# Hybrid trunk: input scaled as its chunks land, the unscaled transposes moved to the output projection, time steps from the normalised input

## Chip, core and metric

One core of one Trainium2 chip runs the whole forward pass in one launch. The metric is the device time of one execution in microseconds. The engines are PE (TensorE), DVE (VectorE), ACT (ScalarE), POOL (GpSimd) and SP (SyncE, which here only issues DMAs; ACT and POOL issue some as well).

## What is computed

The reference, cut to the part that the change touches. SEQ = 1024 tokens and 16 meta tokens ahead of them give L = 1040 rows of D = 1024; the mixer has 32 heads in 4 groups, an inner width of 2048, a state of 128.

```
h = concatenate([meta_tokens, x])                      # 1040 x 1024
u = rmsnorm(h) * ssd_norm
z, xbc, dt_raw = split(u @ w_in)                       # 2048, 2048 + 2*4*128, 32
xbc = silu(causal_conv4(xbc) + conv_b)
dt = softplus(dt_raw + dt_bias);  a = -exp(a_log)
y = chunked_state_space_scan(xbc, dt, a)               # scores cb, decays, states
hg = rmsnorm_per_group(y * silu(z)) * gate_norm
h = h + hg @ w_out                                     # the output projection
...                                                    # conv FFN; K/V; attention; conv FFN; final norm
```

All matrices are float32. A product at nearly full precision is made of three products of rounded operands (`mm3`): each operand is split into a high part rounded to fp32r and a low part, the rest, and high·high, high·low and low·high are summed in PSUM. In the names, `wh`/`wl` are the parts of a weight, `uh`/`ul` those of the normalised input, `yh`/`y` those of the gated scan's output.

## The kernel before

**Tiles.** The rows lie in 9 chunks of 116 (the last 112) tokens, `CH`; three chunks make one of the three time tiles of 348, 348 and 344 columns, `TT`. Features are handled as 8 blocks `k` of 128. After the transposition, features lie on partitions and tokens along the row.

**Front (`load_x`, L327 to L398).** SP and ACT issue the loads of the chunks in turn (L405; odd chunks and the meta tokens on SP, even ones on ACT), and SP that of the dt weight. For each time tile there are two steps, in the order of the table `ORD`. `stream(j)` squares the tile's chunks (L364 on DVE for the chunks in `SQD`, L366 on ACT), transposes the raw chunks (L371, `xT`), copies them out as the residual `hs` (L374 on ACT, L376 on DVE), multiplies them with the dt weight in full fp32 (L377, `dtr`), sends them to memory for the third tile (L379, `h_d`), and forms each row's normalising factor (`token_rstd`, L244 to L250: one step on DVE, Ln and Exp on ACT, four steps on DVE). `scaled(j)` multiplies the chunks by their factors in place (L388), transposes them again (L393, `xr`), and splits them with the norm's gain (`parts`: `uh` L303 on ACT, `ul` L304 on DVE).

**Projections and scan.** `stream` (L603) walks blocks of 128 output columns, three time tiles each: 24 products (`pj`, L193 to L195), then for the blocks that need it the convolution (ACT L320, DVE L323) and a silu that `settle` puts out later. The weight of a block is loaded by SP (L174), its high part made by ACT (L180), its low part by POOL (L98). `dt_path` (L434 to L503) makes the time steps and decay sums from `dtr` while group 0 is projected; it multiplies `dtr` by the rows' factors because `dtr` was made from unscaled input, and sends its tables `acs_d` and `ea_d` to memory, to be read back as `D` and `E`. The scan's first score is `cb` (L665).

**Output projection (`out_proj`, L817).** For groups g = 0, 1, 2 and output blocks f = 0 to 7, `accumulate` sums four `mm3` for each time tile into a bank `acc` and adds it to the residual `h[f]` on DVE (L431). Five banks go round. For g = 0, `fetch` (L419) reads `h[f]` back from `h_d`. For g = 1 and 2, `fetch_y` (L804) reads the group's output from memory and `split_y` scales and splits it (DVE t L813, ACT `yh` L814, DVE `y` L815); group 0's is split ahead by the same lines. At the same time the last group's gate norm ends: PE's column sums of squares `ms` (L226), ACT's Ln and Exp (L229, L230) and DVE's steps L231 to L234, then L579.

**Order.** A scheduler orders the instructions of every engine ahead of time, and the engines carry them out in that order. `behind(x, y)` adds an order only: x is put after y. Within a tile pool a name takes a bank or buffer when its last reader is done; `xT` in the changed kernel, `ms` and `xr` share three banks (`sm`). DMA completions of SP and ACT go through eight semaphores in turn, so a DMA is issued only when the one eight before it has ended.

## Time and profile before

| | |
|---|---|
| median of three runs | 2895.37 us (2894.5 to 2897.03) |
| the profiled execution | 2894.96 us, its span 2893.3 us |
| PE, DVE, ACT, POOL busy in the span | 2834.0, 2092.7, 1628.8, 1631.9 us |
| mean granted clock of PE | 0.996 |
| DMA | 278.70 MB, 96 GB/s over the span |

Busy time is what an engine spent on instructions that are not control or DMA issue. In rows of the timeline the first number is the start in us from the beginning of the span, the second the duration; "x3" is the number of instructions that were put together, and the bracket says how long the engine was idle before and what ended it. Durations of neighbours on one engine overlap where the engine is pipelined, so the step from one start to the next is the price in a row.

### The profile page before, as it was taken

To read this page: it belongs to the slowest core of one execution; us is meant where nothing else is said; L and a number is where in the kernel's file an instruction comes from. 1 tells how busy PE (TensorE), PEld (TensorE's weight loads), DVE (VectorE), ACT (ScalarE), POOL (GpSimd) and SP (SyncE) were. 2 spreads that over 40 slices of the span, in tenths; PEclk is the share of its full clock that TensorE was granted. 3 is DMA by queue.
4 is the path that set the end of the run, shared out by engine and by line. 5 is a ranking of instruction groups with operands and counts; after the bars stand their busy time and mean duration, and the time that the engine had idled before them with its cause. 6 is when DMAs were issued, how large, how long until landed. Compare 5 with 4: busy or idle time off the path is not lost.

```text
span 2893.3 us, 58596 instructions
## 1 busy us (share of the span) xinstructions
PE 2834.0 (98%) x21835; PEld 2704.3 (93%) x21835; DVE 2092.7 (72%) x4032; ACT 1628.8 (56%) x3386; POOL 1631.9 (56%) x2438
## 2 busy tenths in 40 slices
PE   7999999999999999999999999999998999999998
PEld 4999999999989999999999999999798999999888
DVE  5676666668387666667886888888749676767776
ACT  4455544544256555565335888888736565555433
POOL 2275555553538888868853222222364888886882
PEclk9999999999999999999999999999999999999999
DMA  5233333343212222245132222222331222225321
GB/s 168 75 107 94 117 93 117 113 157 134 83 73 82 81 75 81 74 152 178 43 126 78 57 67 66 62 62 55 134 117 66 88 76 79 80 82 183 109 103 66
DMA packets 128265, 278.70 MB, mean 96 GB/s; under 512 B 14787, under 2 KB 58828, under 8 KB 127980
## 3 DMA queue, kind: packets, MB, share of 16 engines
q1 hardware_dynamic: 122028, 261.70, 27.6%
q10 hardware_dynamic: 4112, 6.56, 0.7%
q0 software_dynamic: 1840, 6.70, 0.6%
q8 instruction: 172, 2.82, 0.4%
q14 instruction: 113, 0.93, 0.1%
HBM read 204.63 MB, written 55.36 MB: 90 GB/s over the span
## 4 chain that ended last, share of the span: by engine, by line
PE 87%; DVE 7%; ACT 2%; POOL 2%; DMA 1%; issue 1%; ACTq 0%; DVEq 0%; SPq 0%; POOLq 0%
PE p L193 10%; PE p L195 10%; PE p L194 10%; PE pj L193 8%; PE pj L194 8%; PE pj L195 8%; PE acc L193 7%; PE acc L194 7%; PE acc L195 7%; PE po L1518 3%; PE lg L1477 2%; PE wT L1504 2%; PE y L706 1%; POOL wl L98 1%; DVE bl L978 1%
## 5 line engine op out<-in xcount | busy, mean ns | idle before, releaser
L98 POOL TENSOR_TENSOR wl<-w,wh 128x256 fp32r<-128x256 f32 x780 | 701.0, 929 | 439.4 <-ACT wh L180 298.7
L193 PE MATMUL pj<-uh,wh 128*128 128x348 f32 (+2 forms) x1536 | 500.6, 326 | 2.6 <-DVE qs L1428 1.8
L194 PE MATMUL pj<-ul,wh 128*128 128x348 f32 (+2 forms) x1536 | 495.2, 322 | 0.0
L195 PE MATMUL pj<-uh,wl 128*128 128x348 f32 (+2 forms) x1536 | 492.2, 320 | 0.0
L193 PE MATMUL p<-bh,fh 128*128 128x262 f32 (+1 forms) x1408 | 401.7, 285 | 9.2 <-ACT bh L977 5.9
L195 PE MATMUL p<-bh,fl 128*128 128x262 f32 (+1 forms) x1408 | 401.1, 285 | 3.0 <-POOL fl L98 3.0
L194 PE MATMUL p<-bl,fh 128*128 128x262 f32 (+1 forms) x1408 | 400.5, 285 | 0.9 <-DVE bl L978 0.9
L98 POOL TENSOR_TENSOR fl<-x,fh 128x256 fp32r<-128x256 f32 x352 | 264.8, 783 | 153.1 <-ACT fh L1029 127.3
L194 PE MATMUL p<-bl,wh 128*128 128x262 f32 (+1 forms) x1056 | 299.6, 284 | 2.2 <-DVE bl L978 2.2
L193 PE MATMUL p<-bh,wh 128*128 128x262 f32 (+1 forms) x1056 | 300.7, 285 | 0.4 <-DVE h L431 0.3
L195 PE MATMUL p<-bh,wl 128*128 128x262 f32 (+1 forms) x1056 | 299.5, 284 | 0.0
L193 PEld LDWEIGHTS pj<-uh,wh 128*128 128x128 f32 x1536 | 288.6, 188 | 5.0 <-issue 1.8
L194 PEld LDWEIGHTS pj<-ul,wh 128*128 128x128 f32 x1536 | 289.1, 188 | 1.1
L195 PEld LDWEIGHTS pj<-uh,wl 128*128 128x128 f32 x1536 | 288.8, 188 | 0.6 <-issue 0.6
L323 DVE SCALAR_TENSOR_TENSOR c<-p,params,c 128x260 f32<-128x260 f32 (+1 forms) x528 | 248.4, 480 | 51.0 <-ACT c L320 44.6
L193 PEld LDWEIGHTS p<-bh,fh 128*128 128x128 f32 x1408 | 269.0, 191 | 10.7 <-ACT bh L977 6.8
L195 PEld LDWEIGHTS p<-bh,fl 128*128 128x128 f32 x1408 | 268.4, 191 | 3.4 <-POOL fl L98 3.4
L194 PEld LDWEIGHTS p<-bl,fh 128*128 128x128 f32 x1408 | 268.7, 191 | 1.1 <-DVE bl L978 1.1
L1077 ACT ACTIVATE ft<-p 128x262 f32<-128x262 f32 (+1 forms) x352 | 133.7, 382 | 181.9 <-DVE p L1080 112.1
L195 PE MATMUL acc<-gh,wl 128*128 128x260 f32 (+1 forms) x672 | 213.6, 320 | 2.6 <-POOL wl L98 2.6
L193 PE MATMUL acc<-gh,wh 128*128 128x260 f32 (+1 forms) x672 | 210.9, 320 | 3.2 <-DVE h L1238 3.1
L194 PE MATMUL acc<-gl,wh 128*128 128x260 f32 (+1 forms) x672 | 213.9, 319 | 0.0
(323 smaller groups left out, 7884.9 us busy)
## 6 DMA issues: line engine op xcount, KB each, us to landing
w<-in_w_up SPq DMA_DIRECT2D x88, 512.0 KB
w<-in_w_down SPq DMA_DIRECT2D x44, 512.0 KB
w<-in_w_in SPq DMA_DIRECT2D x40, 512.0 KB
E<-ea_d SPq DMA_DIRECT2D x32, 464.0 KB
D<-acs_d SPq DMA_DIRECT2D x32, 420.5 KB
g<-c SPq DMA_DIRECT2D x88, 130.0 KB
g<-c SPq DMA_DIRECT2D x88, 128.0 KB
b<-g SPq DMA_DIRECT2D x16, 520.0 KB
```

Of the source, the lines that this page charges most:

```text
L98: eng.tensor_tensor(out[:, c], x[:, c], y[:, c], op=op)
L193: self.behind(mm(out, wh, uh, start=first, stop=False, skip_group_check=joins), tie, "behind the sums of squares")
L194: mm(out, wh, ul, start=False, stop=False, skip_group_check=joins)
L195: mm(out, wl, uh, start=False, stop=last, skip_group_check=joins)
L323: ins = nc.vector.scalar_tensor_tensor(out, ps[:, o + i : o + i + n], wcol(i), out, op0=ALU.mult, op1=ALU.add)
L706: nc.tensor.matmul(y, xdt[:n, i, :], dk[:, i, :], start=True, stop=c == 0)
L978: self.last_low = nc.vector.tensor_tensor(hl[1], x, hl[0].bitcast(F32), op=ALU.subtract)
L1077: nc.scalar.activation(s[:, :N], ps[:, :N], AF.Copy)
L1477: nc.tensor.matmul(ps[:nt, :m], part[:, c0 : c0 + nt], ks[a][:, s0 : s0 + m], start=x == 0, stop=x == 1)
L1504: nc.tensor.transpose(pt[:ns, x * CB : x * CB + nt], bt[a][:nt, x * CB : x * CB + ns], self.ident[:nt, :nt])
L1518: nc.tensor.matmul(po[64 * a : 64 * a + 64, :nt], v[: CH[c][1], c, 64 * a : 64 * a + 64], wt[a][: CH[c][1], c, :nt], start=x == 0, stop=x ...
```

## The change

**Front.** The unscaled transposes, their copies, the store of `h_d` and the fp32 `dtr` products go. Chunks 0 and 2 are issued by ACT, the others by SP, with the first weight (`first`) and the dt weight between chunks 1 and 3. A tile's chunks are squared, factors are formed for the first two chunks and for the third apart, each chunk is scaled in place (one half of the third on DVE, the other on ACT), transposed (L400, `xr`) and split as before. `dtr` is made of three products per block from `uh` and `ul`, with the weight's parts in a zero-padded buffer so that all tiles sum into one bank of 96 rows; the factor in `dt_path` goes. The front is now a generator, stepped in turn with the first three blocks' tiles of `stream`, and `hold`, `copy_tie`, `silu_tie` and `last_mm` order silus, weight copies and transposes behind it. The meta tokens are transposed apart (L429) and stored as `meta_d`.

**Output projection.** `residual` (L904) replaces `fetch`: it reads 128 columns of x as 8 x 128 rows of 512 bytes (L911), transposes them on PE (L914, `xT`, three banks of up to 384 columns), copies each bank on ACT (L918) into the place of the residual, reads the meta tokens' columns from `meta_d` (L919), and zeroes the two columns ahead (L920). The lines of `split_y` are now L877 to L879, the add of `accumulate` is L491, L579 is L634, `fetch_y` L868.

```diff
-        nc.scalar.activation(wh[:, :n], w32[:, :n], AF.Copy)
+        self.behind(nc.scalar.activation(wh[:, :n], w32[:, :n], AF.Copy), self.copy_tie, "behind the tiles in front")
...
-    def load_x(self, pool, mx):
+    def load_x(self, pool, mx, first):
...
+        def load(c):
+            t0, n = CH[c]
             xt = pool.tile([P, D], F32, tag="x", name=self.nm("x"), bufs=XB)
             if c == 0:
                 nc.sync.dma_start(xt[:META, :], a["meta"])
                 self.by_rows(nc.scalar, xt[META:n, :], a["x"][: n - META, :], n - META)
             else:
+                self.by_rows(nc.scalar if c == 2 else nc.sync, xt[:n, :], a["x"][t0 - META : t0 - META + n, :], n)
             xs.append(xt)
+        for c in range(3):
+            load(c)
+        w32 = self.wp.tile([P, 1024], F32, tag="w32", name="w32_0")
+        nc.sync.dma_start(w32, first)
+        w0 = [self.wp.tile([P, 1024], F32R, tag=t, name=self.nm(t)) for t in ("wh", "wl")]
+        wdt = self.wp.tile([P, 1024], F32, tag="w32", name="wdt")[:, : KD * H]
+        nc.sync.dma_start(wdt, a["w_dt"])
+        for c in range(3, 9):
+            load(c)
...
+        G = 3 * H
+        wd = [self.Q("wd", F32R) for _ in range(2)]
+        for t in wd:
+            nc.gpsimd.memset(t.bitcast(F32), 0.0)
+        taps = [t[:, 2 * H : 2 * H + KD * G].rearrange("p (k h) -> p k h", h=G)[:, :, :H] for t in wd]
+        made = {}
+        def square(c, tie):
+            n = CH[c][1]
+            t = self.wp.tile([P, D], F32, tag="wl", name=self.nm("junk"))
+            x, acc = xs[c][:n, :], ss[:n, c : c + 1]
+            if c in SQD:
+                ins = nc.vector.scalar_tensor_tensor(t[:n, :], x, 1.0, x, op0=ALU.mult, op1=ALU.mult, accum_out=acc)
+            else:
+                ins = nc.scalar.activation(t[:n, :], x, AF.Square, accum_out=acc)
+            self.behind(ins, tie, "behind the tile in front")
...
+        def factors(j, i, n):
+            self.token_rstd(ss[:, 3 * j + i : 3 * j + i + n], CB, n, y=r9[:, i : i + n, j])
+        def scale(c, parts, tie=None):
+            n = CH[c][1]
+            r = r9[:n, c % 3 : c % 3 + 1, c // 3]
+            for eng, c0, c1 in parts:
+                x = xs[c][:n, c0:c1]
+                if eng is nc.vector:
+                    self.behind(eng.tensor_scalar(x, x, r, None, op0=ALU.mult), tie, "behind the last factors' sums")
+                else:
+                    eng.activation(x, x, AF.Copy, scale=r)
+        def transposed(j, ks):
             s0, nn = TT[j]
+            for k in ks:
+                ps = self.sm("xr")
+                for i, x in enumerate(xs[3 * j : 3 * j + 3]):
+                    n = CH[3 * j + i][1]
+                    t = nc.tensor.transpose(ps[:, i * CB : i * CB + n], x[:n, k * P : k * P + P], self.ident[:n, :n])
+                    if j:
+                        self.behind(t, self.last_mm, "behind the products in front")
+                made[j, k] = self.parts(ps[:, :nn], u[k], s0, nn, self.par("ssd_norm", k))
+        def tile(j):
+            a, b, c = range(3 * j, 3 * j + 3)
+            if j == 0:
+                for x in (a, b, c):
+                    square(x, None)
+            factors(j, 0, 2)
+            scale(a, [(nc.vector, 0, D)])
+            factors(j, 2, 1)
+            scale(b, [(nc.scalar if j else nc.vector, 0, D)], None if j else self.first_factor)
+            if j == 0:
+                self.behind(nc.scalar.activation(w0[0], w32, AF.Copy), self.last_exp, "behind the factors")
+                pieces(nc.gpsimd, w0[1], w32, w0[0].bitcast(F32), ALU.subtract)
+            scale(c, [(nc.vector, 0, D // 2), (nc.scalar, D // 2, D)])
+            transposed(j, range(KD // 2))
+            if j < 2:
+                hi, lo = made[j, KD // 2 - 1]
+                square(a + 3, hi)
+                square(b + 3, lo)
+            transposed(j, range(KD // 2, KD))
+            if j < 2:
+                square(c + 3, made[j, KD - 1][0])
+        pm = self.lg("mT")
+        for k in range(KD):
+            nc.tensor.transpose(pm[:, k * META : k * META + META], xs[0][:META, k * P : k * P + P], self.ident[:META, :META])
+        mt = self.tmp("mT")[:, : KD * META]
+        nc.scalar.activation(mt, pm[:, : KD * META], AF.Copy)
+        nc.sync.dma_start(self.meta_d.rearrange("k p c -> p k c"), mt.rearrange("p (k c) -> p k c", c=META))
+        dt = self.lg("dtr")
+        def steps():
+            tile(0)
+            w = wdt.rearrange("p (k h) -> p k h", h=H)
+            self.behind(nc.scalar.activation(taps[0], w, AF.Copy), made[0, 0][0], "behind the first tile")
+            nc.gpsimd.tensor_tensor(taps[1], w, taps[0].bitcast(F32), op=ALU.subtract)
+            self.behind(nc.scalar.activation(heads[:, 1], heads[:, 1], AF.Exp), made[0, KD - 1][0], "behind the first tile")
+            nc.vector.tensor_scalar(heads[:, 1], heads[:, 1], -1.0, None, op0=ALU.mult)
+            self.hold = True
+            yield
+            for j in range(3):
+                s0, n = TT[j]
+                c = slice(HALO + s0, HALO + s0 + n)
+                for k in range(KD):
+                    w = slice(2 * H + G * k - H * j, 2 * H + G * k - H * j + G)
+                    self.mm3(dt[:G, :n], wd[0][:, w], wd[1][:, w], u[k][0][:, c], u[k][1][:, c], j == k == 0, j == 2 and k == KD - 1, tie=self.last_mm)
+                if j < 2:
+                    tile(j + 1)
+                    self.copy_tie = made[1, 3 + 4 * j][0]
                 else:
+                    self.hold = None
+                self.silu_tie = self.last_exp
+                yield
+        return u, dt, heads, w0, steps()
...
-        tt(v3, pv[R].rearrange("p (c h) -> p c h", h=H), r9[:CB].rearrange("p i j -> p (i j)").unsqueeze(2).to_broadcast([CB, 9, H]), op=ALU.mult)
-        tt(v3, v3, bias, op=ALU.add)
+        tt(v3, pv[R].rearrange("p (c h) -> p c h", h=H), bias, op=ALU.add)
...
+        if self.hold:
+            return
...
-                if i + 1 < len(todo):
-                    w.append(self.load_w(todo[i + 1][0], D))
                 cur = w.pop(0)
+            if j == (late and i == 0) and i + 1 < len(todo):
+                w.append(self.load_w(todo[i + 1][0], D))
...
-            hd, u, *dt = self.load_x(pool, mx)
-            dt = self.dt_path(*dt, mx)
+            u, dt, heads, w0, front = self.load_x(pool, mx, self.a["w_in"][DI // P])
+            dt = self.dt_path(dt, heads, mx)
+            next(front)
+            rows = [[] for _ in range(4)]
+            group = self.stream(self.in_group(u, 0, rows[0]), w0, True)
+            for _ in range(3):
+                next(group)
+                next(front)
+            next(dt)
...
-                    h[f] = self.fetch(hd[f], "h", front=HB)
+                    h[f] = self.residual(f)
...
+    def residual(self, f):
+        nc = self.nc
+        t = self.Q("h")
+        nc.sync.dma_start(t[:, :SEQ].rearrange("p (c q) -> p c q", q=P), self.a["x"][:, f * P : f * P + P].rearrange("(c p) q -> p c q", p=P))
+        banks = [self.sm("xT") for _ in range(3)]
+        for c in range(SEQ // P):
+            nc.tensor.transpose(banks[c // 3][:, c % 3 * P : c % 3 * P + P], t[:, c * P : c * P + P], self.ident)
+        for i, ps in enumerate(banks):
+            n = min(3 * P, SEQ - 3 * P * i)
+            o = HB + META + 3 * P * i
+            nc.scalar.activation(t[:, o : o + n], ps[:, :n], AF.Copy)
+        nc.sync.dma_start(t[:, HB : HB + META], self.meta_d[f])
+        nc.gpsimd.tensor_copy(t[:, :HB], self.zero[:, :HB])
+        return t
```

PE's order at the start. Before, with the second tile's first transposes (`xT`), the last `dtr` product of the first tile, and the first scaled transposes (`xr`):

```order
L377 MATMUL dtr_107<-h_175,wdt 32x348 [waits DVE_49]
L371 MATMUL xT_296<-ident,x_120 128x116 [waits DMAHW2_49,DMAHW0_49,PE_49]
L371 MATMUL xT_296<-ident,x_123 128x116 [waits DMAHW3_49,DMAHW1_49]
L371 MATMUL xT_296<-ident,x_126 128x116 [waits DMAHW6_49,DMAHW4_49]
L377 MATMUL dtr_107<-h_176,wdt 32x348 [waits Activation_49]
L371 MATMUL xT_302<-ident,x_120 128x116 [waits PE_49]
L371 MATMUL xT_302<-ident,x_123 128x116
L371 MATMUL xT_302<-ident,x_126 128x116
L393 MATMUL xr_242<-ident,x_108 128x116 [waits DVE_49]
L393 MATMUL xr_248<-ident,x_108 128x116
L393 MATMUL xr_254<-ident,x_108 128x116
L393 MATMUL xr_242<-ident,x_114 128x116 [waits DVE_49]
```

After, PE's first rows, from the meta tokens' transposes to the first projection product:

```order
L429 MATMUL mT_177<-ident,x_106 128x16 [waits DMAHW0_49,Pool_49]
L429 MATMUL mT_177<-ident,x_106 128x16 x7
L400 MATMUL xr_221<-ident,x_106 128x116 [waits DMAHW3_49,DMAHW1_49,DVE_49]
L400 MATMUL xr_227<-ident,x_106 128x116
L400 MATMUL xr_233<-ident,x_106 128x116
L400 MATMUL xr_221<-ident,x_110 128x116 [waits DMAHW4_49,DMAHW2_49,DVE_49]
L400 MATMUL xr_227<-ident,x_110 128x116
L400 MATMUL xr_233<-ident,x_110 128x116
L400 MATMUL xr_221<-ident,x_113 128x116 [waits DMAHW7_49,DMAHW5_49,DVE_49]
L400 MATMUL xr_227<-ident,x_113 128x116
L400 MATMUL xr_233<-ident,x_113 128x116
L193 MATMUL pj_280<-uh_139,wh_118 128x352 [waits Activation_49]
```

The scaled transposes now open PE's work, each set waiting for its own chunk, and the first projection product stands right behind the first three blocks.

PE's order in the output projection, from the sums of squares of the last gate norm on. Before, where `acc_6989` is the third output block's sum over the second time tile:

```order
L226 MATMUL ms_6825<-z_6269,ones 128x348 [waits DVE_49]
L226 MATMUL ms_6839<-z_6306,ones 128x344 [waits DVE_49,PE_49]
L193 MATMUL acc_6989<-yh_6666,wh_6967 128x348 [waits DVE_49]
L194 MATMUL acc_6989<-y_6484,wh_6967 128x348
L195 MATMUL acc_6989<-yh_6666,wl_6968 128x348
L193 MATMUL acc_6989<-yh_6667,wh_6967 128x348
L194 MATMUL acc_6989<-y_6485,wh_6967 128x348
```

After, where `acc_6936` is the second block's sum over the third tile:

```order
L226 MATMUL ms_6794<-z_6261,ones 128x344 [waits DVE_49,PE_49]
L914 MATMUL xT_6825<-ident,h_6823 128x128 [waits DMAHW6_49,DVE_49]
L914 MATMUL xT_6825<-ident,h_6823 128x128 x2
L914 MATMUL xT_6826<-ident,h_6823 128x128 [waits DVE_49]
L914 MATMUL xT_6826<-ident,h_6823 128x128 x2
L914 MATMUL xT_6827<-ident,h_6823 128x128 [waits Activation_49]
L914 MATMUL xT_6827<-ident,h_6823 128x128
L914 MATMUL xT_6892<-ident,h_6890 128x128 [waits DMAHW7_49,Activation_49]
L914 MATMUL xT_6892<-ident,h_6890 128x128 x2
L914 MATMUL xT_6893<-ident,h_6890 128x128 [waits Activation_49]
L914 MATMUL xT_6893<-ident,h_6890 128x128 x2
L193 MATMUL acc_6936<-yh_6621,wh_6885 128x344 [waits DVE_49]
```

Between the last of these sums of squares and the next sum now stand five sets of the residual's transposes; `xT_6826` takes the bank of `ms_6780`, and `acc_6936` one that an add has to give back.

DVE's order there, ending after the second tile's L232 of that norm. Before:

```order
L231 TENSOR_TENSOR z_6269<-y_6827 128x348 [waits Activation_49]
L813 SCALAR_TENSOR_TENSOR t_7299<-y_7281,params,r_7277 128x348 [waits DMAHW0_49]
L431 TENSOR_TENSOR h_7024<-h_7024,acc_7027 128x348 [waits PE_49]
L815 TENSOR_TENSOR y_7279<-t_7291,yh_7287 128x348 [waits Activation_49]
L431 TENSOR_TENSOR h_7024<-h_7024,acc_7041 128x348 [waits PE_49]
L815 TENSOR_TENSOR y_7280<-t_7295,yh_7288 128x348 [waits Activation_49]
L813 SCALAR_TENSOR_TENSOR t_7303<-y_7282,params,r_7277 128x348 [waits DMAHW1_49,DVE_49]
L232 TENSOR_TENSOR z_6269<-z_6269,ms_6825 128x348 [waits DVE_49]
L431 TENSOR_TENSOR h_7024<-h_7024,acc_7055 128x344 [waits PE_49]
L815 TENSOR_TENSOR y_7281<-t_7299,yh_7289 128x348 [waits Activation_49]
L813 SCALAR_TENSOR_TENSOR t_7307<-y_7279,params,r_7277 128x348 [waits DVE_49]
```

After (two more L877 rows of group 1, `t_7366` and `t_7370`, stand a few rows ahead):

```order
L877 SCALAR_TENSOR_TENSOR t_7374<-y_7356,params,r_7352 128x348 [waits DMAHW1_49]
L879 TENSOR_TENSOR y_7354<-t_7366,yh_7362 128x348 [waits Activation_49]
L879 TENSOR_TENSOR y_7355<-t_7370,yh_7363 128x348 [waits Activation_49]
L877 SCALAR_TENSOR_TENSOR t_7378<-y_7357,params,r_7352 128x348 [waits DMAHW2_49,DVE_49]
L232 TENSOR_TENSOR z_6224<-z_6224,ms_6780 128x348 [waits DVE_49]
L877 SCALAR_TENSOR_TENSOR t_7382<-y_7354,params,r_7352 128x348 [waits DVE_49]
L879 TENSOR_TENSOR y_7356<-t_7374,yh_7364 128x348 [waits Activation_49]
L877 SCALAR_TENSOR_TENSOR t_7386<-y_7355,params,r_7352 128x348 [waits DVE_49]
L233 TENSOR_SCALAR z_6224<-z_6224 128x348 [waits DVE_49]
L879 TENSOR_TENSOR y_7357<-t_7378,yh_7365 128x348 [waits Activation_49]
L877 SCALAR_TENSOR_TENSOR t_7390<-y_7356,params,r_7352 128x348 [waits DVE_49]
L491 TENSOR_TENSOR h_6823<-h_6823,acc_6841 128x348 [waits DMAHW6_49,DMAHW4_49,Activation_49]
```

The adds (L431) that stood between group 1's splits are gone from this stretch; the first add (L491) stands behind them, and it waits for a DMA (`meta_d`) and for ACT (the copy out of `xT_6825`).

86 lines of the change are left out of this document (18 added, 68 removed).

## Prediction

> **What bounds the kernel now.** I read the page first (busy time and the chain of waits), then the windows by stage, then the timelines of each engine in the two stages that the change touches. The page's first group (engine, busy time and its share of the span, instructions) and the chain by engine:
>
> ```profile
> PE 2834.0 (98%) x21835; PEld 2704.3 (93%) x21835; DVE 2092.7 (72%) x4032; ACT 1628.8 (56%) x3386; POOL 1631.9 (56%) x2438
> PE 87%; DVE 7%; ACT 2%; POOL 2%; DMA 1%; issue 1%; ACTq 0%; DVEq 0%; SPq 0%; POOLq 0%
> ```
>
> PE is busy for 98% and carries 87% of the chain. So a change pays where it takes PE work away or shortens a time in which PE has nothing to do, and costs where it makes PE wait. The windows (stretch, length, busy us and instructions of each engine, granted clock, DMA share, GB/s) show where that can be:
>
> ```profile
> core 0: us, PE busy (x) PEld busy (x) DVE busy (x) ACT busy (x) POOL busy (x), PEclk, DMA share, GB/s
> 0.00:20.00 20.00, 5.95 (x17) 2.43 (x18) 4.43 (x17) 6.05 (x12) 4.92 (x28) 1.00 0.93 237
> 20.00:40.00 20.00, 18.00 (x91) 8.76 (x90) 13.44 (x27) 11.72 (x26) 9.67 (x12) 1.00 0.35 107
> ...
> 660.00:680.00 20.00, 20.00 (x125) 19.59 (x124) 17.91 (x35) 12.72 (x22) 8.90 (x10) 1.00 0.18 57
> 680.00:700.00 20.00, 20.00 (x128) 20.00 (x127) 19.96 (x40) 4.89 (x10) 5.58 (x7) 1.00 0.52 178
> ```
>
> The start is the one stage with an idle PE: 5.95 of 20 us, then 18.00. The output projection (from 645 us) keeps PE full, but just there VectorE is nearly full too: 40 instructions in 19.96 us of 680 to 700, 0.50 us each. That stage has no reserve on VectorE.
>
> PE, then ScalarE at the start (start, duration, engine and line, what it does, count, and the idle time before it with what ended it; the first scan product stands last among PE's):
>
> ```profile
> 10.92 1.00 PE L371 MATMUL xT<-ident,x 116*128 116x116 f32 x4 [4.34 <-DMA x<-in_x]
> ...
> 13.66 0.84 PE L371 MATMUL xT<-ident,x 116*128 116x116 f32 x3
> ...
> 22.28 0.52 PE L371 MATMUL xT<-ident,x 116*128 116x116 f32 x3
> 22.73 0.77 PE L377 MATMUL dtr<-h,wdt 128*32 128x348 f32 x2
> ...
> 28.54 0.76 PE L393 MATMUL xr<-ident,x 116*128 116x116 f32 x6
> ...
> 130.74 0.27 PE L665 MATMUL cb<-ident,xbc 128*116 128x128 f32 x1
> ...
> 5.23 9.86 ACTq L405 DMA_DIRECT2D x<-in_x  x5
> 15.20 1.06 ACT L366 ACTIVATE junk<-x 116x1024 f32<-116x1024 f32 x1 [13.11 <-DMA x<-in_x]
> 16.16 0.19 ACT L366 ACTIVATION_READ_ACCUMULATOR junk<-x 116x1 f32 x1
> ...
> 25.03 1.04 ACT L180 ACTIVATE wh<-w 128x1024 fp32r<-128x1024 f32 x1
> ```
>
> ScalarE's queue is held by its x issues until 5.23 + 9.86 = 15.1, so its first square starts at 15.20, although the first chunks had landed by 10.92 (what PE's four transposes waited for). The scaled transposes (L393, `xr`), the first work of the projections, begin at 28.54, and the first scan product (L665, `cb`) at 130.74.
>
> **Front: what goes and what comes.** PE loses 24 dtr products in full fp32 (two records each) and 24 triples of unscaled transposes, 22.73 − 22.28 = 0.45 us for a triple and 0.77 for a product, and gains 72 dtr products at the price of a projection product, which the first and last of 21 such rows give, (102.98 − 99.76)/20 = 0.16 us:
>
> ```profile
> 99.76 0.33 PE L195 MATMUL pj<-uh,wl 128*128 128x352 f32 x1
> ...
> 102.98 0.32 PE L194 MATMUL pj<-ul,wh 128*128 128x352 f32 x1
> ```
>
> That is 24 × 1.22 = 29.3 us out (a part of it in the time that PE had to wait anyway) and 72 × 0.16 = 11.5 in, with 8 transposes of 16 columns for the meta tokens while PE idles. What counts is when the scaled transposes begin. Chunk 2, issued by ScalarE behind chunk 0 before and after, is landed by 10.92. Its square is 1.06 + 0.19 us, to 12.2. Then comes the chunk's factor: VectorE's first step, ScalarE's Ln and Exp, and four steps more on VectorE. The rows for it and for the tile's other work, VectorE and last ScalarE:
>
> ```profile
> 12.21 1.22 DVE L364 SCALAR_TENSOR_TENSOR junk<-x 116x1024 f32<-116x1024 f32 x1
> ...
> 17.42 0.17 DVE L244 TENSOR_SCALAR ss<-ss 116x3 f32<-116x3 f32 x1 [0.40 <-ACT junk L366]
> 19.14 0.16 DVE L247 TENSOR_TENSOR tb<-r 116x3 f32<-116x3 f32 x1 [1.55 <-ACT r L246]
> ...
> 19.74 0.16 DVE L250 TENSOR_TENSOR r<-r,tb 116x3 f32<-116x3 f32 x1
> ...
> 26.24 3.46 DVE L388 TENSOR_SCALAR x<-x,r 116x1024 f32<-116x1024 f32 x3 [0.37 <-PE xT L371]
> ...
> 32.70 1.54 DVE L304 SCALAR_TENSOR_TENSOR ul<-xr,params,uh 128x348 fp32r<-128x348 f32 x3
> ...
> 30.11 1.43 ACT L303 ACTIVATE uh<-xr,params 128x348 fp32r<-128x348 f32 x3 [0.91 <-PE xr L393]
> ```
>
> From L244 to the end of L250 these steps spread over 2.5 us, of which ScalarE spent about 1.0 on another chunk's square; without it about 1.5. So the factor is there at 13.7 and Exp ended 0.8 sooner, at 12.9. ScalarE then copies the first weight (1.04, to 13.95) and scales half of chunk 2 (half of a 1.06 pass, 0.55 as an estimate, to 14.5); with waits between engines I take 15.3 for the third chunk's transposes, which open the projections in place of 28.54.
>
> The first tile is then paced by VectorE, not by PE: 8 low parts (1.54/3 = 0.51 each, 4.1), the square of chunk 4 (1.22), factor steps (5 × 0.17) and the scaling of chunk 3 (3.46/3 = 1.15): 7.3 us behind the first high part (1.43/3) at about 16.1, so the first tile's products end at 23.4. The 24 dtr products take 3.85, to 27.2. The second tile, whose chunk 5 is scaled behind VectorE's first convolution, starts 1.8 later (estimate) and is paced in the same way: 29.0 to 36.3. From there PE has 400 projection products and 48 dtr products at 0.16, 24 transposes at 0.10 ((0.76 − 0.27)/5, taking 0.27 as the latency of one) and 1.5 us of small ones: 64.0 + 7.7 + 2.4 + 1.5 = 75.6, to 111.9. For small waits on ScalarE and VectorE (2.00 us in 20 to 40 before) I add 1 to 4, so `cb` comes at 112.9 to 115.9, taken 114.2: **16.5 us earlier**. The bounds: 12 if chunk 2 or the first weight comes 3 us later and the second tile has a further wait, 19 if tile two hides behind PE. The dt path ends nearer to `cb`, by this sum some 20 us ahead of it; its readers stand behind `cb`, so it costs nothing; had it no such cover, its two round trips through memory would cost some microseconds. The weights of the second and third block, queued behind the chunks, are needed at 31.6 and 36 by the same sum, and I cost their later start at nothing within the bounds given.
>
> **Output projection: what is moved.** The residual, until now read back transposed in eight DMAs, is read as x in 512-byte rows and transposed by PE, 64 transposes, with 24 ScalarE copies, 8 little DMAs for the meta tokens on SP's queue behind weight and y loads, and 8 zero copies. A transpose of 128 columns in a row costs (1.04 − 0.27)/7 = 0.11 us by rows of the last stage, eight in a row and a lone one:
>
> ```profile
> 2857.34 1.04 PE L1643 MATMUL fin<-ident,h 128*128 128x128 f32 x8
> ...
> 2865.64 0.27 PE L1643 MATMUL fin<-ident,h 128*128 128x128 f32 x1
> ```
>
> 64 of them are 7.0 us (7.4 with 0.115), all on a full PE. The larger term is a wait. Rows of before, PE and VectorE, ScalarE, then SP:
>
> ```profile
> 645.03 0.32 PE L193 MATMUL acc<-yh,wh 128*128 128x348 f32 x1
> ...
> 671.04 0.32 PE L194 MATMUL acc<-y,wh 128*128 128x344 f32 x1
> ...
> 659.25 0.52 DVE L815 TENSOR_TENSOR y<-t,yh 128x344 fp32r<-128x344 f32 x1 [0.56 <-ACT yh L814]
> ...
> 664.74 0.96 DVE L231 TENSOR_TENSOR z<-y 128x348 f32<-128x348 f32 x1 [1.41 <-ACT y L230]
> ...
> 663.18 1.14 ACT L180 ACTIVATE wh<-w 128x512 fp32r<-128x512 f32 x2
> 664.22 0.48 ACT L230 ACTIVATE y<-y 128x348 f32<-128x348 f32 x1
> ...
> 641.79 3.70 SPq L419 DMA_DIRECT2D h<-h_d  x8
> ```
>
> Group 0's last y of the third tile is split at 659.25 + 0.52. Before, the adds (L431) run as soon as a sum is there, give their banks back, and PE works through blocks 1 to 3 while VectorE and ScalarE split group 0's y; block 4 starts at 671.04, 144 products after 645.03. After, an add must wait for ScalarE's copy of the transposed residual. PE therefore has only five sums to work on (60 products, 9.6 us); its last one needs that last y, and the next bank is asked for by the transposes. The second triple of them takes the bank of the second square sum, which VectorE gives back with its L232 of that tile, and that row now stands behind six instructions on group 1's y (the order of instructions is shown with the change). PE's order is fixed, so it stands there; and ScalarE's first copy waits for that triple, the first add for the copy, and block 1's last sum for that add.
>
> I price it along VectorE, which sets the pace here. Its L231 starts half a microsecond sooner than 664.74 (one of two weight copies, 1.14/2, now stands behind L230): 664.2. From this row to the add that gives block 4's first sum its bank stand 56 instructions; at 0.50 each 28.0, to 692.2. Against 671.04 that is 21.2 later. Transposes of the first four blocks lie within this wait; the 32 of the last four come on top with 3.7. **Loss 24.9 us**. Bounds: 7.4 if every wait is covered, 21 if VectorE's instructions follow at 0.43, the spacing left when 0.50 loses its overlap, more if x comes late (below). PE is full behind it (20.00 in each window shown), so nothing is won back.
>
> The waits open gaps in PE's work, which the start of before shows as costly: its triple of transposes took 0.84 at 13.66, between pauses, and 0.52 at 22.28. The Trainium skill, "TensorE: Matmul & The Clock Gate", in its part on the HAM clock gate, says that after an idle window of about 3.4 us the array runs at half its clock until it has been busy for as long; the granted clock of 1.00 in the rows shows no such thing, the durations do. By it the 12 products of the first sum after the wait would cost 1.9 us more and the time would be 2905.7; by the rows' sum this stays out, since VectorE sets the pace there anyway.
>
> **Sum.** 24.9 − 16.5 = +8.4 on the profiled run's 2894.96 us (span 2893.3 and 1.66 around it) gives 2903.4; the median, 2895.37, lies 0.41 above that run, so 2903.8. A difference of 0.2%, 5.8 us, is about what can be told from none: faster is below 2889.6, slower above 2901.2.
>
> **Rivals.**
> (1) The waits in the output projection are covered, and only PE's transposes cost: 7.4 − 16.5 = −9.1, 2886.3, faster. For it: VectorE has 2.1 us free in 660 to 680, and its adds before 660 fall away. It decides at a loss of 16.5: block 4 at 671.04 + 12.8 = 683.8, that is 56 VectorE instructions in 19.6 us, 0.35 each, where the rows show 0.50; so it needs PE not to wait for L232 as the order says. Chance 0.18. A half cover (loss 12 to 19, 2891 to 2898) gets 0.15.
> (2) The 512-byte rows are slow. Eight x blocks are 4.19 MB. The nearest rows with short runs (464 bytes, the dt path's) and the h loads:
>
> ```profile
> 102.00:104.00 2.00, 2.00 (x15) 2.00 (x14) 1.56 (x4) 1.16 (x3) 0.87 (x2) 1.00 0.40 89
> ...
> 652.00:658.00 6.00, 5.76 (x35) 5.20 (x34) 5.10 (x12) 1.80 (x4) 0.00 (x0) 1.00 1.03 419
> ```
>
> 89 GB/s at a share of 0.40 would be 222 at full share (estimate): x landed 18.9 us after 641.8, at 660.7, and y 2.13 MB at 419 GB/s later, at 665.8, in time for VectorE, which comes to the last y at about 671.7. At 100 GB/s y lands at 688.8 and all shifts by 17, to 2920. It decides at 169 GB/s. Chance 0.10. The Trainium skill, "DMA: Bandwidth & Descriptors", in its table of specifications, puts the smallest transfer for full rate at 512 B; by that x would be in at the rate of h and this rival void; no run shown here has such rows.
> (3) The front gives only 10 to 12 (the first weight or chunk 2 late, the second tile waiting): 2908 to 2910. Chance 0.10.
>
> **How the numbers follow.** The forecast itself, 2897 to 2909 from the bounds of both terms, has 0.47, about a tenth of it (0.05) within 0.2%. Rival (1) and a fifth of its half cover give faster 0.21; the rest of the half cover and that tenth give same 0.17; the rest of the forecast and the rivals (2) and (3) give slower 0.62. The range runs from the first rival's 2886 to 2914, leaving out the faster half of (1) and the slow half of (2).
>
> **What would show it.** Right: `xr` at about 15, `cb` at about 114; in the output projection PE idle ahead of the residual's second triple of transposes, released by L232, and block 4's first sum 47 us behind the first `acc` (26.0 before). Wrong: PE busy through that stage (first rival), x or y as releaser of VectorE's L877 (second), or a `cb` later than 118 (third).

## The result, and the profile after

The changed kernel took 2906.4 us (median of 5 runs, 2905.42 to 2909.34) against 2895.37 (5 runs beside them, 2894.5 to 2897.08): a ratio of 1.0037, 95% interval 1.0026 to 1.0049, or 7.5 to 14.2 us more. Forecast were 2903.8 us and +8.4. The profiled execution took 2905.42 us, its span 2903.7.

First the page's busy times, then the windows of the front and of the output projection (stretch, length, busy us and instructions of each engine, granted clock, DMA share, GB/s).

```profile
PE 2832.6 (98%) x21859; PEld 2716.7 (94%) x21859; DVE 2085.3 (72%) x4032; ACT 1638.5 (56%) x3411; POOL 1624.9 (56%) x2440
```

```profile
0.00:20.00 20.00, 6.72 (x29) 5.14 (x30) 7.63 (x26) 9.54 (x20) 9.79 (x34) 1.00 0.91 238
20.00:40.00 20.00, 18.67 (x121) 17.15 (x120) 14.15 (x40) 15.83 (x35) 4.58 (x7) 1.00 0.43 133
...
640.00:660.00 20.00, 8.13 (x29) 5.58 (x28) 15.25 (x33) 13.75 (x26) 2.22 (x4) 0.72 0.52 172
660.00:680.00 20.00, 20.00 (x130) 19.78 (x129) 18.33 (x38) 8.33 (x20) 8.56 (x10) 0.94 0.20 56
680.00:700.00 20.00, 20.00 (x135) 19.95 (x134) 4.91 (x10) 5.69 (x15) 4.88 (x9) 1.00 0.16 43
...
649.10:676.70 27.60, 19.77 (x118) 18.20 (x116) 27.35 (x57) 15.71 (x33) 8.90 (x10) 0.81 0.19 51
```

PE's busy total hardly moved (2834.0 to 2832.6), so the 10 us are a matter of when it may work. The front has little more PE time in its first 40 us (25.4 against 23.95), but it is useful work earlier. The new hole is 640 to 660: PE busy 8.13 of 20. The last row is the stretch that the forecast priced along VectorE: 57 instructions, busy 27.35 of 27.60 us. Behind it, in 680 to 700, VectorE is at 4.91 where it was at 19.96 before: its work wasn't more (2085.3 us in the whole run, 2092.7 before), it had to be done before PE could go on.

The front in the timelines of PE and ScalarE (start, duration, engine, line, what, count, idle time before and what ended it):

```profile
11.58 0.84 PE L400 MATMUL xr<-ident,x 116*128 116x116 f32 x3 [5.90 <-DVE x L390]
14.58 0.84 PE L400 MATMUL xr<-ident,x 116*128 116x116 f32 x3 [2.16 <-DVE x L390]
15.75 0.84 PE L400 MATMUL xr<-ident,x 116*128 116x116 f32 x3 [0.32 <-DVE x L390]
16.84 0.66 PE L193 MATMUL pj<-uh,wh 128*128 128x352 f32 x1 [0.25 <-ACT uh L303]
...
24.99 0.32 PE L193 MATMUL dtr<-uh,wd 128*96 128x348 f32 x1
...
30.25 0.42 PE L193 MATMUL pj<-uh,wh 128*128 128x352 f32 x1 [0.44 <-ACT uh L303]
...
38.01 0.32 PE L195 MATMUL pj<-uh,wl 128*128 128x352 f32 x1
...
115.65 0.27 PE L722 MATMUL cb<-ident,xbc 128*116 128x128 f32 x1
...
12.53 1.06 ACT L375 ACTIVATE junk<-x 116x1024 f32<-116x1024 f32 x1 [2.65 <-DMA x<-in_x]
```

The third chunk's scaled transposes stand at 15.75 (28.54 before for the first of all), the first tile's products end at 24.99, the second tile runs from 30.25 to 38.2, and the first scan product comes at 115.65, **15.1 us earlier** than 130.74. It stays so to the output projection, whose first product stands at 630.20 (645.03 before, 14.8 earlier).

The output projection, PE and then VectorE:

```profile
630.20 0.32 PE L193 MATMUL acc<-yh,wh 128*128 128x348 f32 x1
...
644.58 0.42 PE L193 MATMUL acc<-yh,wh 128*128 128x344 f32 x1 [4.03 <-ACT z L599]
...
647.64 1.84 PE L226 MATMUL ms<-z,ones 128*128 128x348 f32 x4
650.55 0.55 PE L914 MATMUL xT<-ident,h 128*128 128x128 f32 x3 [1.06 <-DVE z L232]
657.13 0.90 PE L914 MATMUL xT<-ident,h 128*128 128x128 f32 x3 [6.04 <-DVE z L232]
...
660.64 0.64 PE L193 MATMUL acc<-yh,wh 128*128 128x344 f32 x1
...
676.77 0.41 PE L193 MATMUL acc<-yh,wh 128*128 128x348 f32 x1
...
649.18 0.76 DVE L231 TENSOR_TENSOR z<-y 128x348 f32<-128x348 f32 x1 [2.15 <-ACT y L230]
...
656.57 0.51 DVE L232 TENSOR_TENSOR z<-z,ms 128x348 f32<-128x348 f32 x1
...
659.58 0.51 DVE L491 TENSOR_TENSOR h<-h,acc 128x348 f32<-128x348 f32 x1
```

PE's second triple of residual transposes waits 6.04 us for VectorE's L232, the first add stands at 659.58, and block 4's first sum starts at 676.77, **46.57 us behind the first `acc`** (26.01 before). Then the distance still grows by 3.5 us: the 577th product (group 2's first) stands 118.44 us behind the first, before 94.33. So the projection lost 24.1 us to there. The spans add up: the first `acc` 14.8 us earlier, the last product of group 2 24.4 later behind it (163.98 for 139.56), and 0.8 more from there to the end make the 10.4 between 2893.3 and 2903.7.

### The profile page after: what moved, and what is told of

Its sections match the earlier page's. It is cut to its first block, busy times and chain, and to the rows that moved or that the text cites. A ratio compares the mean times of both kernels' runs of the same rounds, so it can differ in the third digit from the quotient of the medians.

```text
span 2903.7 us, 58710 instructions
## 1 busy us (share of the span) xinstructions
PE 2832.6 (98%) x21859; PEld 2716.7 (94%) x21859; DVE 2085.3 (72%) x4032; ACT 1638.5 (56%) x3411; POOL 1624.9 (56%) x2440
## 4 chain that ended last, share of the span: by engine, by line
PE 42%; DVE 4%; ACT 2%; POOL 1%; issue 1%; DMA 0%; DVEq 0%; ACTq 0%; SPq 0%; POOLq 0%
PE p L195 5%; PE p L194 5%; PE p L193 5%; PE acc L193 4%; PE acc L194 4%; PE acc L195 4%; PE pj L193 3%; PE pj L195 3%; PE pj L194 3%; PE po L1599 3%; PE lg L1558 2%; PE wT L1585 2%; POOL wl L97 1%; DVE kp L1571 1%; DVE p L1285 0%
```

## The experiments

Each was run beside the kernel before on the same chip. The marks are counted in PE's timeline: the first scan product, then block 4's first sum (product 145) and group 2's first product (577), both from the first `acc` product, and the idle time of PE in 620 to 700 that its rows name. The kernel before took 2896.44 us beside E1 to E4, 2896.5 beside E5 to E8, 2895.88 beside E9 and 2895.27 beside E10. E5, E7 and E8 are single runs, of which the marks say more than the times.

| | median us | ratio to before, 95% | scan product | 145th | 577th | idle |
|---|---|---|---|---|---|---|
| before | 2895.37 | | 130.74 | 26.01 | 94.33 | 0.61 |
| after | 2906.4 | 1.0037, 1.0026 to 1.0049 | 115.65 | 46.57 | 118.44 | 12.33 |
| E1 front alone | 2878.12 | 0.9935, 0.9921 to 0.995 | 115.52 | 25.96 | 94.33 | 0.65 |
| E2 projection alone | 2921.48 | 1.0086, 1.007 to 1.0103 | 130.27 | 47.01 | 118.8 | 11.65 |
| E3 group 1's split later | 2905.6 | 1.003, 1.002 to 1.0041 | | 45.82 | 116.81 | 9.95 |
| E4 no transposes | 2878.2 | 0.9935, 0.9921 to 0.995 | | 25.98 | 94.59 | |
| E5 long rows | 2905.39, one run | | 115.98 | 46.57 | 118.46 | |
| E6 transposes in `acc` | 2889.86 | 0.9973, 0.9962 to 0.9983 | 116.3 | 29.87 | 101.69 | 2.07 |
| E7 dummies in front | 2907.21, one run | | 116.16 | | | |
| E8 dummies in the wait | 2906.75, one run | | 116.17 | 47.18 | 118.97 | 8.68 |
| E9 residual added later | 2893.72 | 0.9992, 0.9983 to 1.0001 | 115.62 | 25.95 | 101.43 | 0.65 |
| E10 E9, copies on ScalarE | 2897.72 | 1.0011, 1.0002 to 1.002 | 116.06 | 26.36 | 100.56 | 1.98 |

### E1 and E2: each half by itself

E1 is the new front with the residual read as before, from a transposed copy that the front stores; the copy is of the normalised rows' high part, in place of x, so that no unscaled transposes are needed.

```diff
+                    for k in range(KD):
+                        nc.sync.dma_start(self.h0_d[k], u[k][0][:, HALO : HALO + L].bitcast(F32))
...
-                    h[f] = self.residual(f)
+                    h[f] = self.fetch(self.h0_d[f], "h", front=HB)
```

> The changed kernel with the old read of the residual (eight contiguous loads); what is stored for it is the high part of the normalised input, so the residual's values are not the reference's, and no transposes of x stand in the output projection. Theory (the front gains, the output projection loses, and the two add): cb at about 115.7 as in the changed kernel, block 4's first sum 26 us behind the first acc, 2880.5 us (2878.5 to 2882.5), 14.9 below the kernel before. Rival, that a part of the front's gain is given back further on: cb at 115.7, but 2884 us or more.

E2 is the old kernel with the new `residual`:

```diff
-                    h[f] = self.fetch(hd[f], "h", front=HB)
+                    h[f] = self.residual(f, hd)
```

> The kernel before with the new residual alone (x in 512-byte rows, transposes on PE, copies on ACT; the meta columns come from the stored input). Theory: cb at 130.7, block 4's first sum 46 to 47 us behind the first acc, 2920.6 us (2918 to 2923), 25 above the kernel before. Rival, that the loss comes from the two parts meeting (loads or small DMAs shifted against each other): under 2915.

E1: 2878.12 beside 2896.44, 18.3 less and a little below the range expected; E2: 2921.48 beside the same, 25.0 more. So each half does by itself about what it does in the whole; their sum, +6.7, lies a little below the interval of the whole (+7.5 to +14.2); single executions of one kernel spread over 4 to 5 us, so that is not resolved. E1's first scan product is 15.2 earlier; the 3 us beyond it are within the same spread. What E1's windows show of the projection is the point of the case:

```profile
640.00:660.00 20.00, 20.00 (x123) 19.27 (x122) 16.44 (x32) 12.52 (x22) 6.92 (x8) 1.00 0.39 140
660.00:680.00 20.00, 20.00 (x128) 20.00 (x127) 20.00 (x42) 6.55 (x13) 6.08 (x7) 1.00 0.32 98
```

VectorE is as full as ever (20.00 of 20 in 660 to 680) and PE stays at 20.00: as long as an add needs only its own sum, the backlog stays on VectorE. So the full VectorE is not what costs; it costs once PE's next bank hangs on the end of its queue.

### E4 and E5: the rows of x, or the transposes

E4 reads the same 512-byte rows straight into the residual's place, untransposed (so the residual is x in the wrong arrangement), without transposes and copies.

```diff
-        nc.sync.dma_start(t[:, :SEQ].rearrange(...), self.a["x"][...])
-        banks = [self.sm("xT") for _ in range(3)]
...
+        nc.sync.dma_start(t[:, HB : HB + SEQ].rearrange(...), self.a["x"][...])
```

> The changed kernel, in which x is read in its 512-byte rows straight into the place of the residual; its transposes and copies are left out (the residual's values are not the reference's). Theory (the short rows themselves cost nothing, the waits and PE's transposes do): block 4's first sum 26 to 28 us behind the first acc, 2881 to 2883 us. Rival, that x and behind it y land too late in short rows: 33 us or more behind the first acc, 2888 or more.

E5 keeps transposes and copies and reads rows of 4 KB of a weight in place of x:

```diff
-        nc.sync.dma_start(t[:, :SEQ].rearrange("p (c q) -> p c q", q=P), self.a["x"][...])
+        nc.sync.dma_start(t[:, :SEQ], self.a["w_in"][f])
```

> The changed kernel with the residual's blocks read from another input of the same size in 4 KB rows (the values are not the reference's), transposes, copies and adds as they were. Theory (short rows cost nothing, since y is read before VectorE comes to it): loads at some 400 GB/s in place of 290, but block 4's first sum still 46 to 47 us behind the first acc. Rival (x and y land late in short rows): under 42 us.

E4 gives all of E1's time with the short rows in it (2878.2, below the 2881 to 2883 expected, 145th product at 25.98), E5 nothing. The DMA view of 636 to 665 in 40 slices, after and then E5:

```profile
GB/s 291 289 291 289 291 292 289 290 297 344 383 436 407 419 413 419 402 121 0 0 0 96 264 13 0 0 0 0 0 0 0 0 23 0 11 0 0 0 0 0
```

```profile
GB/s 412 435 390 427 379 437 384 442 396 430 396 430 121 0 0 0 0 23 0 0 0 14 189 170 0 0 0 0 0 0 0 0 0 0 5 6 0 0 0 0
```

The short rows go at about 290 GB/s, where others go at 400 and more, and it doesn't matter: x is in before anybody asks for it. The whole loss hangs on the transposes and copies.

### E3 and E8: whose pace

E3 orders group 1's y splitting behind block 1's adds, so that L232 no longer stands behind it.

```diff
+            if g == 1:
+                self.behind(ins, self.tie_add, "behind the adds")
```

> The changed kernel with one order added: the splits of group 1's y come on VectorE behind the adds of blocks 0 and 1. Theory (the row L232, which gives back the bank for the second triple of transposes, stands behind group 1's splits): PE waits 3 us for it in place of 6.0, block 4's first sum comes 43 to 44 us behind the first acc in place of 46.6, and the time is 2903 to 2904. Rival, that x in short rows is what is waited for: 46.6 and 2906.4 as in the changed kernel.

E8 fills PE's long wait with 36 transposes that nobody reads, to keep its clock up.

```diff
+            if f == 0 and c == 2:
+                for i in range(36):
+                    nc.tensor.transpose(banks[0][:, 3 * P :], self.ident, self.ident)
```

> The changed kernel with 36 transposes of the identity on PE within the 6 us in which it waits for L232 in the output projection, into columns that nobody reads. Theory (the pauses leave PE's clock at half, and from 660 us on PE is what ends last): granted clock near 1.00 from 657 us on, the first sum behind the wait at 0.16 us a product in place of 0.235, block 4's first sum 45 to 46 us behind the first acc in place of 46.6. Rival (VectorE's adds set the pace up to block 4): faster products, but 46.4 or more.

PE's waits in 620 to 720 (what waits, for whom, us in total, times, longest), after and then E3:

```profile
PE xT L914 <- DVE z L232: 7.1, 2, 6.0
```

```profile
PE xT L918 <- DVE z L232: 4.6, 2, 3.5
```

E3's VectorE (L232 of the norm's second tile, then the splitting that was put off):

```profile
653.87 0.52 DVE L232 TENSOR_TENSOR z<-z,ms 128x348 f32<-128x348 f32 x1
...
663.61 4.57 DVE L877 SCALAR_TENSOR_TENSOR t<-y,params,r 128x348 f32<-128x348 f32 x8
668.10 0.50 DVE L491 TENSOR_TENSOR h<-h,acc 128x348 f32<-128x348 f32 x1
```

E3 takes 2.5 us from the wait for L232 and gets 0.75 of it at the 145th product (45.82 for 46.57) and 1.6 at the 577th; its time of 2905.6 can't be told from 2906.4. The row named as releaser was the right one. What is left of its wait, 3.5, is the norm's own steps, as no splitting stands ahead of L232 any more. Most of the gain is lost again to the splitting that was put off: eight L877 in a row now stand ahead of the next add. The expected 43 to 44 was too much. An order with all of group 1's splitting behind group 0's adds wasn't tried, so how much of the loss is the amount of VectorE's work and how much its order is not shown.

E8 was to show the same from PE's side. The windows of its wait, after first (the clock is the number after POOL's):

```profile
650.00:654.00 4.00, 0.55 (x3) 0.31 (x3) 3.93 (x9) 3.93 (x8) 1.05 (x2) 0.76 0.28 68
654.00:658.00 4.00, 0.87 (x3) 0.50 (x3) 4.00 (x10) 1.69 (x4) 0.00 (x0) 0.50 0.00 0
658.00:662.00 4.00, 3.27 (x14) 2.84 (x14) 4.00 (x10) 2.73 (x8) 1.44 (x1) 0.50 0.04 6
```

```profile
650.00:654.00 4.00, 2.94 (x27) 2.89 (x27) 3.90 (x9) 3.93 (x6) 1.61 (x3) 1.00 0.27 68
654.00:658.00 4.00, 1.89 (x18) 1.65 (x16) 4.00 (x9) 1.90 (x5) 0.00 (x0) 1.00 0.00 0
658.00:662.00 4.00, 3.16 (x15) 2.36 (x14) 4.00 (x11) 2.52 (x7) 0.18 (x1) 0.70 0.02 2
...
660.97 0.49 PE L195 MATMUL acc<-yh,wl 128*128 128x344 f32 x1
```

With the dummies the granted clock stays at 1.00 through 658, where after fell to 0.50. But 2.11 us of waiting were left behind them, and the clock fell after all (0.70 in 658 to 662): the products of the first sum still go at 0.28 to 0.29 us, as the last row shows (the next starts at 661.25). So the products that were to become faster did not, and block 4 starts no sooner (47.18): E8 doesn't show what a faster PE would do. What speaks against a gain is VectorE's share, 4.00 of 4 us from 654 on in both and 27.35 of 27.60 in the whole stretch.

### E7: the clock in the front

E7 puts 44 such transposes ahead of the front's.

```diff
+        for i in range(44):
+            nc.tensor.transpose(warm[:, :P], self.ident, self.ident)
```

> The changed kernel with 44 more transposes of the identity on PE at the start, behind those of the meta tokens and ahead of the first chunk's; nobody reads them. They take one of the three banks for a while. Theory (PE's slow first products are those of a gated clock, and they set the pace of the first tile): its transposes take 0.52 us for three in place of 0.84 and its products 0.16 each in place of 0.29, and cb comes at 114.2 to 115.0 in place of 115.65. Rival (VectorE sets the pace of the first tile): faster products, but cb at 115.5 or later.

```profile
5.61 6.62 PE L432 MATMUL warm<-ident 128*128 128x128 f32 x44
...
15.07 0.52 PE L400 MATMUL xr<-ident,x 116*128 116x116 f32 x3 [2.74 <-DVE x L390]
...
17.95 0.84 PE L400 MATMUL xr<-ident,x 116*128 116x116 f32 x3
```

The first triple after them takes 0.52 where after's took 0.84, but the slow pace is back by 17.95, behind the pauses of 2.74 and 0.65 us, and the scan product comes at 116.16, later than after by as much as chunk 2 is (13.02 for 12.53). Inconclusive: the pace of the first tile wasn't changed for long enough.

### E6, E9 and E10: getting the residual in another way

E6 transposes into the `acc` bank ahead of the products and lets these run on, so that neither copies nor adds of the residual are left. Other than its expectation has it, the residual doesn't come out whole in its result (why is not shown), so its time is that of the order of work alone.

```diff
-                    h[f] = self.residual(f)
+                    h[f], xs = self.residual(f)
+                    for j in range(3):
+                        self.added(h[f], xs, j, w, ops, next(banks))
```

> The changed kernel, but x is transposed straight into each sum's bank, three transposes of 116 columns ahead of its products, and VectorE copies the finished sum out: no copies on ScalarE, no wait of an add for a copy, no bank of its own, no stored meta columns. The result is the reference's. Theory (what is lost is the wait; PE's transposes alone cost about 0.10 us each, 72 of them 7.2): block 4's first sum 29.5 to 31 us behind the first acc, group 0's end 56 us behind it (48.9 before, 73.0 after), and the time 7 to 8 us below the kernel before, 2888 to 2890. Rival (PE now waits for x itself, since the transposes stand first): 3 us or more of idle PE at the first blocks, block 4's first sum 33 us or more behind, no gain over the kernel before.

```profile
630.91 0.26 PE L933 MATMUL acc<-ident,h 116*128 116x116 f32 x1
633.24 0.57 PE L933 MATMUL acc<-ident,h 116*128 116x116 f32 x2 [2.07 <-DMA h<-in_x]
...
634.50 0.49 PE L194 MATMUL acc<-yh,wh 128*128 128x348 f32 x1
```

No transpose waits for a bank of the norm and no add for a copy any more, and of 24.1 us 7.4 are left at the 577th product: the transposes, and some 1.5 of slow products, as the first 11 go at 0.29 each instead of 0.16. PE loses another 2.6 ahead of the first product, where x lands late (the 2.07 wait).

E9 adds the residual in groups 1 and 2, half a block each; group 0 only copies its sums out.

```diff
+        if new:
+            self.nc.vector.tensor_copy(h[f][:, o], ps[:, :n])
...
+        ps = self.sm("xT")
+        for c in range(4):
+            nc.tensor.transpose(ps[:, c * P : c * P + P], v[:, c * P : c * P + P], self.ident)
+        nc.vector.tensor_tensor(h[:, o], h[:, o], ps, op=ALU.add)
```

> The changed kernel with the residual added later: group 0's sums are copied into h by VectorE, and x comes in half blocks of 512 tokens with the weights of groups 1 and 2 (into the unused half of the weight's buffer), is transposed into one bank by four transposes and added there by one VectorE instruction of 512 columns; the meta columns are added by a small one in group 0. All of the transposes stay, no copies on ScalarE, no add waits for x. Theory (what is lost beside PE's transposes is the wait): block 4's first sum 26 us behind the first acc, group 0's end 48.9, the end of group 1 98 us (94.3 before) and the products' end of group 2 147 (139.7 before), and the time 7 to 8 us below the kernel before, 2888 to 2890. Rival (VectorE's 16 more instructions of 512 columns make it the bound in groups 1 and 2): group 2's end at 152 us or more, 2893 or more.

```profile
694.38 4.97 DVE L881 SCALAR_TENSOR_TENSOR t<-y,params,r 128x348 f32<-128x348 f32 x8
699.28 0.50 DVE L495 TENSOR_TENSOR h<-h,acc 128x344 f32<-128x344 f32 x1
...
700.73 3.98 DVE L883 TENSOR_TENSOR y<-t,yh 128x348 fp32r<-128x348 f32 x7
...
701.84 1.03 PE L927 MATMUL xT<-ident,w 128*128 128x128 f32 x8
705.68 0.43 PE L194 MATMUL acc<-yh,wh 128*128 128x344 f32 x1 [2.80 <-DVE h L495]
```

The wait of group 0 is gone (145th product 25.95, as before), but a smaller one has come: at 705.68 (outside the table's stretch) PE has waited 2.80 us for an add that stands on VectorE behind group 2's splitting, seven L883 in a row and, some rows ahead, eight L881. The 577th product stands at 101.43, not the expected 98, and the time cannot be told from before. It lies in the rival's range, but group 2's products end at 150.1, short of the 152 that the rival had.

E10 moves E9's 24 copies to ScalarE, to see whether VectorE's amount of work makes that wait.

```diff
-            self.nc.vector.tensor_copy(h[f][:, o], ps[:, :n])
+            self.nc.scalar.activation(h[f][:, o], ps[:, :n], AF.Copy)
```

> The kernel with the residual added in groups 1 and 2, with one line changed: the 24 copies of group 0's sums out of their banks run on ScalarE in place of VectorE. Where that kernel loses 10.6 us in the output projection, 2.8 of it is one wait at 702 to 705.7: TensorE asks for a bank whose add stands on VectorE behind 16 instructions of the last group's y. Theory (VectorE's backlog of that stage is what is left of the wait): 24 x 0.5 = 12 us leave VectorE, the wait goes, and of the loss only the transposes and small gaps stay, 7.3 to 8; 577th product 98 to 99 us behind the first (101.4 there, 94.3 before), time 2890 to 2891. Rival (the order of VectorE's work, not its amount, makes the wait, since those 16 instructions are put ahead of the add whatever else VectorE does): the 577th product stays at 101 and the time at 2893 to 2894. Second rival (ScalarE now holds the banks, since its copies stand behind its high parts and weight splits): a wait on ScalarE's copies shows by 690 and the time is over 2895.

```profile
680.00:700.00 20.00, 18.30 (x122) 18.01 (x121) 14.58 (x28) 7.23 (x15) 6.51 (x7) 1.00 0.72 238
...
695.99 2.66 DVE L883 TENSOR_TENSOR y<-t,yh 128x348 fp32r<-128x348 f32 x6
698.57 0.93 DVE L495 TENSOR_TENSOR h<-h,acc 128x348 f32<-128x348 f32 x2
...
699.13 0.43 PE L194 MATMUL acc<-yh,wh 128*128 128x344 f32 x1 [1.70 <-DVE h L495]
```

VectorE now has 5.4 of 20 us free in 680 to 700, and PE still waits 1.70 there, for an add behind six L883: this speaks for the order, the first rival, with the splitting issued in one piece ahead of the add. The theory fell. The time is that of the second rival, but its sign didn't come: no wait of PE for a ScalarE copy stands in 625 to 725. What put E10 at 2897.72 is open: its profile shows 3.4 us of PE waits after the projection, for POOL's low part (2.4) and a ScalarE high part (1.0), that E9's has not, but the profile of before has them too (2.49 at 866.25 and 1.09 at 863.00), so they aren't E10's own. E9 in turn is 15.6 above E1 where the projection shows 10.6. By their profiles the rest, 4.7, lies behind the projection: from the last product of group 2 to the end 2114.05 us stand in E9, 2109.30 in E1. That distance is 2106.1 in E4 and 2109.5 in after, so a part of it is spread between executions; its cause is open. No version tried here that keeps x itself as the residual is measurably faster than before; an order that also puts group 2's splitting behind those adds wasn't tried.

## Why the prediction was right

**The bound.** PE's busy time moved by 1.4 us only. As argued, it came down to the front's idle time and to the projection's coupling to VectorE. The total, +11.0 by the medians for +8.4, is no case of two errors that cancel: the front gave 1.4 less than forecast, the projection cost about what was forecast, and 0.8 came behind it.

**Front, 16.5 forecast, 15.1 measured.** The chunk's path was right in its steps and 0.45 us late at the third chunk (15.75 for 15.3), since chunk 2 landed at 12.53, not 10.92. The first tile ended at 24.99, not 23.4, the second ran from 30.25 to 38.2, not 29.0 to 36.3. The mis-sized term is the first tile's pace, 9.2 us from 15.75 for the 8.1 of the sum: the products go at 0.29 and the triples at 0.84 until 20.48, then at 0.16 and 0.46. The sum had VectorE pace this tile; in 17 to 19 PE is the full engine (2.00 of 2 us, VectorE 1.54). What the tile takes at full pace no run shows. From 38.2 to the scan product stand 77.5 us where the sum had 77.9. The dt path nearer to its readers cost nothing: from scan product to first `acc` 514.55 us, before 514.29.

**Projection, 24.9 forecast, 24.1 to the 577th product and 25.0 in E2.** The step that carried it was right nearly to the number: from L231 (649.18, that is 18.98 behind the first `acc`; forecast 19.2) to block 4's first sum 27.6 us with 57 instructions, forecast 28.0 with 56. The bank that PE asks for is given back by L232, as read from the order. Not priced is one wait ahead of it: 4.0 us for ScalarE's `z`, behind three of its high parts of group 0's last tile, before the fifth sum, the one that the prediction names as waiting for that tile; L231 is not later for it (18.98 behind the first `acc`, 19.71 before). What follows block 4 gave 3.5, forecast 3.7 for the other 32 transposes.

**The rivals.** (1), waits covered, fell with the 6.04 us at 657.13, and its half cover with a loss of 24; its price of 7.4 is what E6 shows where no add waits for a copy. (2), slow rows: 290 GB/s, below the 419 of the h loads but above its point of 169, no row of VectorE's L877 waits for a load in that stage, and E5 settles it. (3), a front of 10 to 12, fell with 15.1.

**The clock.** Here the granted clock shows what the rows of before did not: 0.50 in 654 to 662 and 0.96 in 662 to 666, so about half of the first sum after the wait ran slow, 2.75 us for its 12 products where 0.16 each makes 1.9. The Trainium skill, "TensorE: Matmul & The Clock Gate", in its part on the HAM clock gate, says that an idle window halves the clock. By it the forecast would have been 1.9 us higher. The trace agrees that the clock is halved in a wait, but sooner than after the 3.4 us that the prediction takes from it: the wait began at 651.09 and 652 to 654 reads 0.52 already. Leaving the 1.9 out rests on VectorE, as the prediction says: busy for 27.35 of 27.60 us from L231 to block 4, it had 0.25 us in which a faster PE could have helped. That is argued from this row; E8 doesn't test it. The 1.00 in the rows of the start, which the prediction set against the durations, was no reading: the trace of before holds its first clock record at 20.84 us, and a window without a record is shown as 1.00.

## What to carry to other kernels

When an operand of an accumulation's last step (here the residual) is given one more producer on another engine, the step inherits that engine's queue, and PE's bank with it: count the instructions from the row that frees the first bank to the one that frees the next. A full engine off the chain cost nothing in E1; once the order made the bound one wait for it, its backlog was paid at once (20.6 us to block 4 here, the transposes of four blocks included). Moving work out of an idle stage into a full one has to be priced in the full one: the front's gain of 15 us went there.

## What was not expected

- Rows of 512 bytes load at about 290 GB/s where 4 KB rows go at some 410 (after and E5 in the same stretch, above).
- Transposes count as work for PE's clock here: with 36 of them the granted clock stays at 1.00 in 650 to 658, where it fell to 0.76 and 0.50 without (E8's windows above, one run).
- A granted clock of 1.00 can be a gap in the record. These are windows of the changed kernel in the front and behind the 4 us wait, and one of E7; products go at 0.29 us each in all three (18.42 to 18.71, 646.21 to 646.50 and 18.91 to 19.20 in the timelines), against 0.16 elsewhere, beside a clock of 1.00 in the first and of 0.50 in the others:

```profile
17.00:19.00 2.00, 2.00 (x7) 1.61 (x8) 1.54 (x4) 1.64 (x5) 2.00 (x3) 1.00 1.03 268
646.00:648.00 2.00, 2.00 (x8) 1.98 (x7) 0.52 (x1) 1.97 (x3) 0.00 (x0) 0.50 1.01 412
...
17.00:19.00 2.00, 2.00 (x9) 1.44 (x8) 1.51 (x3) 1.64 (x5) 2.00 (x4) 0.50 1.04 287
```

  The changed kernel's trace holds its first clock record at 20.62 us, E7's at 8.93. So before 20 us the durations tell the pace, not the 1.00.
